# A hybrid decoder block on one core: the recurrence's loads issued by ScalarE's queue, and the first transfers in another order

## The chip, the core and the metric

The kernel runs on one core of one Trainium2 chip. A core has TensorE (matrix products, written into the eight banks of PSUM), VectorE, ScalarE, GpSimd and SyncE, each with an instruction stream of its own that is worked off in order, and 16 DMA engines that move data between the chip's main memory and the on-chip memory (SBUF). An instruction that moves data is issued from an engine's stream: it waits there for its semaphores, hands the transfer over, and the engine goes on. The metric is the device time of one execution in microseconds (us), lower is better.

## What is computed

One layer on 1024 tokens of width 1024, all in float32: a norm, one input projection, two groups of heads (attention and a gated recurrence), an output projection, a norm, a gated feed-forward part, a last norm. Cut to what matters here:

```python
def rmsnorm(x, w):
    y = x * lax.rsqrt(jnp.mean(x * x, axis=-1, keepdims=True) + NORM_EPS)
    return y * w

u = rmsnorm(h, norm1_w[l])                       # (1, 1024, 1024)
proj = jnp.einsum('bsd,de->bse', u, w_in[l])     # 3584 columns: qa ka va | qb fb ib gb

# group B: 4 heads, state 128x128, chunked
f = lb + (1.0 - lb) * jax.nn.sigmoid(f_logit);  key = 1.0 - f;  qf = jax.nn.silu(q)
S_t = diag(f_t) S_{t-1} + key_t i_t^T;          o_t = S_t^T qf_t
o = o * lax.rsqrt(jnp.mean(o * o, axis=-1) + NORM_EPS)
yb = o * norm_w * jax.nn.silu(g)

h = h + concat(ya, yb) @ w_out;  h = h + ffn(rmsnorm(h, norm2_w));  return rmsnorm(h, final_norm_w)
```

## The kernel before

The kernel does every large product in three reduced-precision parts (each operand is split into a high part `wh` and a rest `wl`), and arranges the large products in Strassen's scheme (seven products in place of eight, hence the sums of halves on VectorE). TensorE has work for nearly the whole span; everything else is made to keep it supplied.

**Who sets the order.** The kernel's code does not issue instructions: `P.op` and `P.flex` record operations with their cost, their reads and their writes, and `Prog.schedule` then lists them engine by engine by their class (`P.cls`, a lower number goes first) and by the length of what still hangs on them. Changing one operation's queue or class can so move any other. Each transfer is recorded by `dma(...)` (L267 to L272), in the kernel before always on SyncE's stream (SP). The built program gives every transfer one of eight completion semaphores in turn, so a transfer also waits, at its issue, for the landing of the one that is eight places before it.

**The start** (L658 on). The eight token tiles `xs[0]` to `xs[7]` (128 tokens each, 512 KB, in the tiles `E0`, `E1`, `E14`, `E15`) are loaded. `norm_rows` squares a tile on ScalarE, takes the root on GpSimd and multiplies by the root and by the norm's weights `w1b` in two halves on VectorE. `w1b` (`wh7`, `wl7`) is the weight vector repeated on all 128 partitions, loaded by two transfers that read the same 2 KB for each partition (256 KB each). `blocks` transposes the normed tile on TensorE against `ident` (64 KB, loaded too) and splits it into the operands of the input projection. From the second tile on, `begin` starts the projections `F0` and `K1` early (DENSE lists the order of the twelve projections), with weights loaded into `st0` and `st1`. `consts()` (L627 on) loads masks and works out the recurrence's bounds `lg`, with an exponential on ScalarE.

**The recurrence.** `hgrn(h)` (L840 on) runs four times, in class 0, among the last input projections. Each head loads four arrays that the projections have written to main memory: `f` (`f_d`), the queries (`q_d`), the values `iv` (`i_d`) and, near its end, the gate `gt` (`g_d`), 512 KB each. All heads share the tiles `E14` (f and keys), `E15` (queries) and `E16` (the score matrix `A` and the values); `gt` overwrites `A`. A head ends with eight squares (ScalarE), a root (GpSimd), eight scaled copies (ScalarE), a transposition (TensorE), a product with the gate (VectorE, L305) and two stores to `m_d`. Behind the recurrence comes the attention (class 1), which fetches its operands from `qs_d`, `kh_d`, `kl_d` and `v_d` with SP's transfers, then the output projection, the feed-forward part and the last norm.

Of the kernel before, what the change touches and what calls it, by code (L numbers as in the profile page):

```python
# [246 lines left out]
def hymba_block(ctx: ExitStack, tc: tile.TileContext, x, norm1_w, w_in, lb_logits, hgrn_norm_w, w_out,  # L247
# [15 lines left out]
    def moved(nbytes, run):  # L263

        return nbytes / run * (0.008 + run / 27e3) / 16

    def dma(o, i, nbytes, run=2048):  # L267
        r = [i] if isinstance(i, (View, Buf)) else []
        w = [o] if isinstance(o, (View, Buf)) else []
        gi = i if r else (lambda: i)  # L270
        go = o if w else (lambda: o)
        P.op("SP", 0.5, lambda: nc.sync.dma_start(go(), gi()), r, w, nbytes=moved(nbytes, run))  # L272

# [83 lines left out]
    def bcast(w, n):  # L357
        return bass.AP(tensor=w.tensor, offset=w.offset, ap=[[0, 128], [1, n]])
# [72 lines left out]
    def slot(tag):  # L431
        return whole(P.buf(tag, [128, 512]))
# [219 lines left out]
    def src_of(w):  # L652
        c = COL[w[0]] + int(w[1]) * 256
        return w_in_v[:, :, c:c + 256], w[0] in "QK"
# [4 lines left out]
    for t in range(NT):  # L659
        if t == 0:  # L660
            for i in range(4):
                dma(xs[i], x[i * 128:(i + 1) * 128, :], 128 * D * 4, 4096)
                if i == 0:
                    for k in range(2):
                        dma(w1b[k], bcast(norm1_w[:, k * 512:k * 512 + 512], 512), 128 * 512 * 4)
                    dma(ident, eye, 65536)
        if t == 2:
# [3 lines left out]
        u = us[t % 2]  # L671
        norm_rows(xt, w1b, u, u, "a")
        blocks(t, u, R, "n", tmp4)
# [10 lines left out]
        if t >= 3 and len(leads) < LEAD:  # L684
            w = seq[len(leads)]
            leads[w] = next(begin(R, *src_of(w), "d", slot(T8[4 + len(leads)]), 7))
    consts()

    csn = E(16, [128, 2048])
# [134 lines left out]
    def hgrn(h):  # L824
# [17 lines left out]
        def blocked(v, w):  # L842
            return sub(v, lambda a: a.rearrange("p c (b e) -> p c b e", e=w))
        dma(f, f_d.v(lambda b: b[rs, :], h), 128 * S * 4)
        dma(qc(0, 128), q_d.v(lambda b: b[rs, :].rearrange("p (c e) -> p c e", e=128), h), 128 * S * 4, 512)
        dma(r128(iv), i_d.v(lambda b: b.rearrange("(c p) n -> p c n", p=128)[:, :, rs], h // 2), 128 * S * 4, 512)

# [91 lines left out]
        gt = A  # L939
        dma(gt, g_d.v(lambda b: b[rs, :], h), 128 * S * 4)  # L940
        ss = P.buf("hss", [128, NT])
# [437 lines left out]
```

## Time and profile before

| | us |
|---|---|
| median of 3 runs | 1258.24 (1257.98 to 1258.44) |
| the profiled execution's own time | 1256.03 |
| its span, first to last instruction | 1254.2 |
| TensorE busy in the span | 1212.3 (97%) |
| VectorE busy | 1028.3 (82%) |
| ScalarE busy | 476.9 (38%) |
| GpSimd busy | 112.0 (9%) |

A busy share is a mean over stages with different limits, so the stages are read one by one. Product records on TensorE overlap and their ends are modelled, so "busy" is not the same as full pace. The feed-forward part, from about 625 us to the end, keeps TensorE busy without a gap. The stages in front of it are where its time is lost.

### The profile page before, as it was taken

What the parts mean: (1) busy time and instruction counts of PE and PEld (TensorE: products, weight loads), DVE (VectorE), ACT (ScalarE), POOL (GpSimd) and SP (SyncE); (2) the same over time, 40 slices, a digit from 0 to 9 for tenths busy, and PEclk for the clock granted to TensorE, in tenths of its full rate; (3) what the DMA queues carried; (4) which work ended last, traced back from release to release, by engine and by line L of the source; (5) the groups of instructions that cost most, each with busy time, mean ns of one, the idle gap of its engine ahead of it and who ended that gap; (6) DMA issues with size and microseconds to landing.
All of it is one profiled execution on the core that took longest, in us unless ns stands there. A gap on an engine that the chain in (4) does not pass through costs nothing.

```text
span 1254.2 us, 17960 instructions
## 1 busy us (share of the span) xinstructions
PE 1212.3 (97%) x6244; PEld 1030.7 (82%) x6244; DVE 1028.3 (82%) x2110; ACT 476.9 (38%) x1020; POOL 112.0 (9%) x212
## 2 busy tenths in 40 slices
PE   4999999999998899999999999999999999999997
PEld 4878889888987788987888888888888887888885
DVE  6999989999789999966888676676676769968986
ACT  5642332344327887842722132221222223223222
POOL 1110000101003433420100000000000000000001
PEclk9999999999999999999999999999999999999998
DMA  8434443514468753316223322323322369434433
GB/s 264 133 127 160 176 147 101 182 68 160 132 195 272 203 143 88 93 54 199 79 76 126 118 97 89 126 85 109 126 84 101 112 230 386 170 101 127 135 109 118
DMA packets 132890, 175.57 MB, mean 140 GB/s; under 512 B 18496, under 2 KB 85696, under 8 KB 132800
## 3 DMA queue, kind: packets, MB, share of 16 engines
q1 hardware_dynamic: 132800, 174.43, 42.4%
q8 instruction: 49, 0.80, 0.3%
q14 instruction: 41, 0.34, 0.1%
HBM read 122.76 MB, written 51.64 MB: 139 GB/s over the span
## 4 chain that ended last, share of the span: by engine, by line
PE 78%; DVE 9%; DMA 7%; ACT 2%; issue 1%; SPq 0%; POOL 0%; DVEq 0%; POOLq 0%; ACTq 0%
PE b L280 76%; DVE wl L301 2%; DVE E L301 2%; PE b L1048 2%; DMA st<-in_w_in_dram 1%; DVE E L864 1%; DVE wh L301 1%; PE b L286 1%; DMA m_d<-lm 1%; DMA st<-in_w_out_dram 1%; DMA E<-kl_d 1%; DVE E L305 1%; DMA i_d<-wl 1%; DVE st L301 1%; ACT wh L337 1%
## 5 line engine op out<-in xcount | busy, mean ns | idle before, releaser
L280 PE MATMUL b<-E,wh 128*128 128x512 f32 (+1 forms) x2096 | 643.6, 389 | 5.1 <-ACT wl L337 1.9
L280 PEld LDWEIGHTS b<-E,wh 128*128 128x128 f32 x2096 | 386.3, 188 | 85.5 <-DVE E L301 4.0
L280 PE MATMUL b<-E,wl 128*128 128x512 f32 (+1 forms) x1048 | 403.9, 385 | 0.0
L347 ACT ACTIVATE wh<-st 128x512 fp32r<-128x512 f32 (+1 forms) x207 | 129.4, 629 | 384.6 <-PE b L280 217.1
L301 DVE TENSOR_TENSOR wl<-st,wh 128x512 fp32r<-128x512 f32 (+1 forms) x340 | 229.5, 685 | 5.3 <-ACT wh L347 2.1
L280 PEld LDWEIGHTS b<-E,wl 128*128 128x128 f32 x1048 | 197.1, 188 | 40.7
L301 DVE TENSOR_TENSOR E<-b,E 128x512 f32<-128x512 f32 (+1 forms) x157 | 105.5, 683 | 39.6 <-PE b L280 37.3
L349 DVE TENSOR_SCALAR wh<-st 128x512 fp32r<-128x512 f32 x119 | 50.0, 423 | 88.0 <-PE b L280 84.6
L280 PE MATMUL b<-wl,wh 128*128 128x512 f32 x308 | 119.9, 389 | 0.5 <-DVE wl L301 0.5
L280 PE MATMUL b<-wh,wl 128*128 128x512 f32 x308 | 119.9, 389 | 0.1
L280 PE MATMUL b<-wh,wh 128*128 128x512 f32 x308 | 119.8, 389 | 0.0
L280 PE MATMUL b<-wl,E 128*128 128x256 f32 (+1 forms) x544 | 116.3, 287 | 2.7 <-DVE wl L301 2.6
L301 DVE TENSOR_TENSOR wl<-b,wl 128x512 f32<-128x512 f32 (+2 forms) x139 | 89.6, 651 | 14.8 <-PE b L280 12.2
L280 PE MATMUL b<-E,E 128*128 128x192 f32 (+3 forms) x464 | 99.6, 324 | 2.0 <-DVE E L305 1.0
L301 DVE TENSOR_TENSOR st<-st 128x512 f32<-128x512 f32 x136 | 92.5, 684 | 0.7
L280 PEld LDWEIGHTS b<-wl,E 128*128 128x128 f32 x544 | 88.0, 191 | 5.8 <-DVE wl L301 3.4
L337 ACT ACTIVATE E<-E 128x512 f32<-128x512 f32 (+2 forms) x77 | 54.2, 704 | 93.5 <-DVE E L301 42.5
L280 PE MATMUL b<-wh,E 128*128 128x256 f32 x448 | 89.1, 290 | 0.2 <-DVE wh L301 0.2
L280 PEld LDWEIGHTS b<-E,E 128*128 128x128 f32 x464 | 75.0, 192 | 8.0 <-issue 2.6
L349 POOL TENSOR_SCALAR wh<-st 128x512 fp32r<-128x512 f32 (+1 forms) x16 | 11.1, 692 | 747.6 <-PE b L280 668.3
L280 PEld LDWEIGHTS b<-wh,E 128*128 128x128 f32 x448 | 72.4, 192 | 0.8 <-DVE wh L301 0.4
L280 PEld LDWEIGHTS b<-wl,wh 128*128 128x128 f32 x308 | 57.8, 188 | 13.0 <-DVE wl L301 0.9
(140 smaller groups left out, 1391.7 us busy)
## 6 DMA issues: line engine op xcount, KB each, us to landing
st<-in_w_gate_up_dram SPq DMA_DIRECT2D x22, 1024.0 KB, 5.2
st<-a_d SPq DMA_DIRECT2D x77, 256.0 KB, 2.8
st<-in_w_in_dram SPq DMA_DIRECT2D x16, 1024.0 KB, 5.7
a_d<-E SPq DMA_DIRECT2D x45, 256.0 KB, 2.1
E<-in_w_down_dram SPq DMA_DIRECT2D x44, 256.0 KB, 5.3
E<-in_x_dram SPq DMA_DIRECT2D x8, 512.0 KB, 9.1
E<-qs_d SPq DMA_DIRECT2D x32, 128.0 KB, 3.9
E<-kh_d SPq DMA_DIRECT2D x32, 128.0 KB, 3.6
```

The lines of the kernel that those rows point to most:

```text
L280: nc.tensor.matmul(o(), lt(), rh(), start=st, stop=sp, skip_group_check=True)
L286: nc.tensor.transpose(ov(), iv(), ident())
L301: P.flex(alts, lambda e: ENG[e].tensor_tensor(o(), a(), b(), op=op), [a, b], [o])
L305: lambda e: nc.vector.scalar_tensor_tensor(o(), a(), s(), b(), op0=op0, op1=op1), [a, s, b], [o])
L337: nc.scalar.activation(o(), a(), func, **kw)
L347: nc.scalar.activation(o(), i(), AF.Copy)
L349: ENG[e].tensor_scalar(o(), i(), 1.0, 0.0, op0=OP.mult, op1=OP.add)
L864: nc.vector.copy_predicated(Av, mv, ps()[:, :, a:a + 64].rearrange("p c (b e) -> p c b e", e=w))
L1048: nc.tensor.transpose(ov(), iv(), ident())
```

## The change

Two edits, and what the scheduler makes of them.

1. `dma` takes a queue; the four loads of each of the four heads are recorded on ScalarE's stream in place of SP's.
2. At the start, the first tile, then the two halves of the norm's weights as one row each (2 KB), then `ident`, are recorded in class 0, ahead of all else. A product of a row of ones with each half on TensorE spreads the weights over 128 partitions into a PSUM bank. The first tile multiplies by that bank directly; ScalarE copies it to `w1b` for the other seven. The tiles 1 to 3 come behind. `consts()` gets class 3, the last.

```diff
-    def dma(o, i, nbytes, run=2048):
+    def dma(o, i, nbytes, run=2048, queue="SP"):
...
-        P.op("SP", 0.5, lambda: nc.sync.dma_start(go(), gi()), r, w, nbytes=moved(nbytes, run))
+        e = {"SP": nc.sync, "ACT": nc.scalar}[queue]
+        P.op(queue, 0.5, lambda: e.dma_start(go(), gi()), r, w, nbytes=moved(nbytes, run))
...
-            for i in range(4):
+            P.cls = 0
+            w1p = []
+            dma(xs[0], x[0:128, :], 128 * D * 4, 4096)
+            dma(ident, eye, 65536, 512)
+            rows = [P.buf(x, [1, 512]) for x in T8[:2]]
+            ones = P.buf("ones", [1, 128])
+            for k in range(2):
+                dma(rows[k], norm1_w[:, k * 512:k * 512 + 512], 2048)
+            P.op("DVE", 0.1, lambda: nc.vector.memset(ones(), 1.0), [], [ones])
+            for k in range(2):
+                ps = bank("d")
+                mm([(whole(ps), whole(ones), whole(rows[k]), True, True, 512, 128, True)], [ones, rows[k]], [ps])
+                P.cls = 2
+                act(w1b[k], whole(ps), AF.Copy, 512)
+                P.cls = 0
+                w1p.append(whole(ps))
+            P.cls = 2
+            for i in range(1, 4):
                 dma(xs[i], x[i * 128:(i + 1) * 128, :], 128 * D * 4, 4096)
-                if i == 0:
-                    for k in range(2):
-                        dma(w1b[k], bcast(norm1_w[:, k * 512:k * 512 + 512], 512), 128 * 512 * 4)
-                    dma(ident, eye, 65536)
...
-        norm_rows(xt, w1b, u, u, "a")
+        norm_rows(xt, w1b if t else w1p, u, u, "a")
...
+    P.cls = 3
     consts()
+    P.cls = 2
...
-        dma(f, f_d.v(lambda b: b[rs, :], h), 128 * S * 4)
+        dma(f, f_d.v(lambda b: b[rs, :], h), 128 * S * 4, queue="ACT")
...
-        dma(gt, g_d.v(lambda b: b[rs, :], h), 128 * S * 4)
+        dma(gt, g_d.v(lambda b: b[rs, :], h), 128 * S * 4, queue="ACT")
```

The queries' and the values' loads change in the same way as `f`.

**The start on SP.** Before, the two repeated halves (`wh_70`, `wl_72`) stand third and fourth, the weights of K1 (`st_74`) ahead of `ident`:

```order
L272 DMA E_67<-in_x_dram 128x1024 x2
L272 DMA wh_70<-in_norm_w_dram 128x512
L272 DMA wl_72<-in_norm_w_dram 128x512
L272 DMA st_74<-in_w_in_dram 128x8x256
L272 DMA E_76<-in_x_dram 128x1024
L272 DMA ident<-in_eye_dram 128x128
L272 DMA st_80<-in_w_in_dram 128x8x128
L272 DMA E_76<-in_x_dram 128x1024
L272 DMA E_86<-in_x_dram 128x1024 x2
```

The same place now, on SP, with two rows of 2 KB in place of the two halves and `st_92` for the weights of F0:

```order
L273 DMA E_67<-in_x_dram 128x1024
L273 DMA wh_71<-in_norm_w_dram 1x512
L273 DMA wh_73<-in_norm_w_dram 1x512
L273 DMA ident<-in_eye_dram 128x128
L273 DMA E_67<-in_x_dram 128x1024
L273 DMA E_78<-in_x_dram 128x1024
L273 DMA st_80<-in_w_in_dram 128x8x256
L273 DMA E_78<-in_x_dram 128x1024
L273 DMA E_86<-in_x_dram 128x1024
L273 DMA st_92<-in_w_in_dram 128x8x128
```

`ident` moved from behind K1's weights and the third tile to the fourth place; the second and third tile now stand ahead of K1's weights, and the fifth ahead of F0's.

**The passage from head 2 to head 3.** SP before, where `E_1666<-f_d` is head 3's load, `E_1756<-g_d` head 2's gate, and the rest fetches the attention's operands and its mask:

```order
L272 DMA E_1647<-q_d 128x8x128
L272 DMA E_3099<-qs_d 32x1024 x4
L272 DMA E_3099<-kh_d 32x1024 x3
L272 DMA E_1666<-f_d 128x1024
L272 DMA E_3099<-kh_d 32x1024
L272 DMA E_3163<-in_amask_dram 128x1920
L272 DMA E_3170<-kl_d 32x1024 x4
L272 DMA E_3194<-qs_d 32x1024 x4
L272 DMA E_1756<-g_d 128x1024
```

ScalarE now, around head 2's gate; `E_1766,hss<-b` are the squares, `E_1766<-b,rsh` the scaled copies, `E_1657` head 3's queries:

```order
L338 ACTIVATE E_1657<-E_1657 128x4x64
L338 ACTIVATE E_1766,hss<-b_3154 128x128
L338 ACTIVATE E_1766,hss<-b_3191 128x128
L338 ACTIVATE E_1766,hss<-b_3154 128x128
L338 ACTIVATE E_1766,hss<-b_3191 128x128
L338 ACTIVATE E_1766,hss<-b_3154 128x128
L338 ACTIVATE E_1766,hss<-b_3191 128x128
L338 ACTIVATE E_1766,hss<-b_3154 128x128
L338 ACTIVATE E_1766,hss<-b_3191 128x128
L273 DMA E_1766<-g_d 128x1024
L338 ACTIVATE E_1657<-E_1657 128x4x64
```

And a little ahead of that, around head 3's load of `f` (`E_1676<-b` are the last copies that head 2 writes into the same tile):

```order
L338 ACTIVATE E_1676<-b_3112 128x512
L338 ACTIVATE E_1676<-b_3121 128x512
L273 DMA E_1676<-f_d 128x1024
L348 ACTIVATE wh_3173<-st_2449 128x512
L338 ACTIVATE wl_3204<-b_2884 128x512
```

The gate's load moved from behind SP's fetches of the mask, of `kl_d` and of `qs_d` to right behind the eighth square, and head 3's load of `f` from behind seven of them to right behind head 2's last copies into its tile.

**The bounds of the recurrence.** ScalarE now, at the first results of F0 (`wh_562<-b` is the first sigmoid, `lg<-lg` the exponential of `consts()`):

```order
L338 ACT_TABLE_LOAD
L338 ACTIVATE wh_562<-b_216 128x512
L348 ACTIVATE E_526<-b_570 128x4x128
L338 ACTIVATE wl_593<-b_516 128x512
L338 ACT_TABLE_LOAD
L338 ACTIVATE lg<-lg 128x8
L348 ACTIVATE E_526<-b_604 128x4x128
L338 ACTIVATE wh_651<-b_198 128x512
L348 ACTIVATE wh_666<-st_387 128x512
L348 ACTIVATE E_526<-b_648 128x4x128
L348 ACTIVATE wh_675<-st_607 128x512
L338 ACTIVATE E_681<-b_516 128x512
```

ScalarE before, at the same place (`wh_573<-b` is the first sigmoid):

```order
L347 ACTIVATE wh_567<-st_312 128x512
L337 ACT_TABLE_LOAD
L337 ACTIVATE wh_573<-b_176 128x512
L337 ACTIVATE wl_595<-b_527 128x512
L347 ACTIVATE wh_607<-st_312 128x512
L337 ACTIVATE wh_622<-b_229 128x512
L347 ACTIVATE wh_651<-st_617 128x512
L337 ACTIVATE wh_639<-wh_639 128x512
```

Before, the exponential stood far ahead, under the table that ScalarE loads first; now it has moved in between the sigmoids, with a table load ahead of it and another behind. The program has 11 table loads in place of 9. Elsewhere the places of the four heads among the projections, and the order of the output projection, the feed-forward part and the end, are nearly those of before; the attention's operations are interleaved a little differently.

## Rows read from the trace of the kernel before

**Rows 1.** Stretches: length; PE, PEld, DVE, ACT, POOL busy; granted clock, DMA share, GB/s

```profile
50.00:75.00 25.00, 24.72 (x114) 20.26 (x113) 21.44 (x35) 12.22 (x20) 6.42 (x5) 1.00 0.30 110
...
1075.00:1100.00 25.00, 25.00 (x112) 20.71 (x111) 23.33 (x43) 6.86 (x11) 0.00 (x0) 1.00 0.34 105
...
8.00:26.00 18.00, 10.66 (x58) 9.79 (x59) 14.11 (x27) 9.99 (x20) 2.82 (x5) 1.00 1.09 356
...
336.00:350.00 14.00, 12.12 (x83) 11.00 (x81) 3.45 (x10) 5.70 (x27) 1.98 (x2) 0.88 1.01 276
350.00:400.00 50.00, 46.07 (x340) 43.59 (x341) 48.88 (x143) 24.78 (x70) 9.60 (x19) 1.00 0.70 225
```

**Rows 2.** Timeline of the start: start us, us, engine, instruction [idle before, releaser]

```profile
4.47 1.06 ACT L337 ACTIVATE E<-E 128x1024 f32<-128x1024 f32 x1 [2.47 <-DMA E<-in_x_dram]
...
7.52 0.75 DVE L305 SCALAR_TENSOR_TENSOR E<-E,rsa,wh 128x512 f32<-128x512 f32 x1 [1.72 <-DMA wh<-in_norm_w_dram]
9.18 0.75 DVE L305 SCALAR_TENSOR_TENSOR E<-E,rsa,wl 128x512 f32<-128x512 f32 x1 [0.84 <-DMA wl<-in_norm_w_dram]
...
12.19 0.63 ACT L347 ACTIVATE wh<-st 128x512 fp32r<-128x512 f32 x1 [5.20 <-DMA st<-in_w_in_dram]
...
13.90 3.65 PE L286 MATMUL b<-ident,E 128*128 128x128 f32 x16 [13.90 <-DMA ident<-in_eye_dram]
...
15.53 0.43 DVE L349 TENSOR_SCALAR wh<-st 128x512 fp32r<-128x512 f32 x1 [1.44 <-DMA st<-in_w_in_dram]
...
22.38 1.03 PE L286 MATMUL b<-ident,E 128*128 128x128 f32 x8
```

**Rows 3.** The chain that ended last, at the start: start us, us, what

```profile
18.12 9.85 DMA st<-in_w_in_dram
...
29.68 2.32 PE b L280 x13
```

**Rows 4.** SP's transfers between head 2 and head 3 (timeline)

```profile
331.34 3.55 SPq L272 DMA_DIRECT2D E<-kh_d  x3
335.07 0.34 SPq L272 DMA_DIRECT2D E<-f_d  x1
...
336.40 1.86 SPq L272 DMA_DIRECT2D E<-kl_d  x4
338.36 5.30 SPq L272 DMA_DIRECT2D E<-qs_d  x4
343.91 0.34 SPq L272 DMA_DIRECT2D E<-g_d  x1
```

**Rows 5.** TensorE, VectorE and ScalarE in the same place (timeline)

```profile
331.25 1.79 PE L280 MATMUL b<-E,E 128*128 128x128 f32 x14
...
340.04 0.69 DVE L301 TENSOR_TENSOR E<-E,E 128x512 f32<-128x512 f32 x1 [3.63 <-DMA E<-f_d]
...
341.12 0.26 ACT L337 ACTIVATE E<-b 128x128 f32<-128x128 f32 x1
...
343.02 0.25 ACT L337 ACTIVATION_READ_ACCUMULATOR E<-b 128x1 f32 x1
...
349.96 0.75 DVE L305 SCALAR_TENSOR_TENSOR E<-b,hw,E 128x512 f32<-128x512 f32 x1 [5.65 <-DMA E<-g_d]
```

**Rows 6.** VectorE's waits from 175 to 430 us: us in total, times, longest

```profile
DVE E L305 <- DMA E<-g_d: 5.6, 1, 5.6
DVE E L301 <- DMA E<-f_d: 3.6, 1, 3.6
```

**Rows 7.** ScalarE: its table loads as a group, and rows near them

```profile
L337 ACT ACT_TABLE_LOAD x9 | 11.5, 1283 | 5.2 <-DMA f_d<-wl 4.4 <-PEq L1365 0.7
...
54.39 1.28 ACT L337 ACT_TABLE_LOAD   x1
55.69 0.60 ACT L337 ACTIVATE wh<-b 128x512 f32<-128x512 f32 x1
...
64.26 0.63 ACT L347 ACTIVATE wh<-st 128x512 fp32r<-128x512 f32 x1 [4.40 <-DMA st<-in_w_in_dram]
```

More of the change, by code (lines that the diff above doesn't have):

```diff
@@ L843, in blocked @@
             return sub(v, lambda a: a.rearrange("p c (b e) -> p c b e", e=w))
-        dma(f, f_d.v(lambda b: b[rs, :], h), 128 * S * 4)
-        dma(qc(0, 128), q_d.v(lambda b: b[rs, :].rearrange("p (c e) -> p c e", e=128), h), 128 * S * 4, 512)
-        dma(r128(iv), i_d.v(lambda b: b.rearrange("(c p) n -> p c n", p=128)[:, :, rs], h // 2), 128 * S * 4, 512)
+        dma(f, f_d.v(lambda b: b[rs, :], h), 128 * S * 4, queue="ACT")
+        dma(qc(0, 128), q_d.v(lambda b: b[rs, :].rearrange("p (c e) -> p c e", e=128), h), 128 * S * 4, 512, "ACT")
+        dma(r128(iv), i_d.v(lambda b: b.rearrange("(c p) n -> p c n", p=128)[:, :, rs], h // 2), 128 * S * 4, 512, "ACT")
         def scores(n, g):
```

## The prediction

> **What bounds the kernel now.** Read the table of stretches first: where TensorE is busy all of its 25 us, as at 1075 us, only fewer or faster products could help. It is short of work at the start (10.66 of 18 us from 8 to 26 us) and from 336 to 350 us (12.12 of 14 us, at a mean granted clock of 0.88, so that part of it ran at the lower of the two levels) [rows 1]. The change touches these two places, so each is read from its timeline.
>
> At the start the DMA engines are the limit: their share is 1.09 from 8 to 26 us, at 356 GB/s [rows 1]. What is wanted comes late: the norm's two weight halves at 7.52 and 9.18 us, K1's weights at 12.19, `ident`, for which the first product waits, at 13.90, F0's at 15.53 [rows 2]. The chain of waits goes on through a lot of weights issued at 18.12 that lands 9.85 us later, behind all that is queued, and reaches TensorE at 29.68 [rows 3]. From 336 to 350 us VectorE, the engine nearest to its limit around there, is busy 3.45 of 14 us [rows 1]. It waits 3.63 us for head 3's `f` and 5.65 us for head 2's gate [rows 5], the only loads in its list of waits from 175 to 430 us [rows 6]. SP's rows show why: both loads stand behind fetches for the attention that take 3.55 and 5.30 us to issue [rows 4].
>
> **The change part by part.** *The first transfers.* The two repeated halves are gone. The second arrives 1.66 us after the first [rows 2], and half a megabyte in all would take 1.5 us at the stretch's mean rate [rows 1]; so they hold the engines between 1.5 us and 2 x 1.66 = 3.3 us. Everything behind them lands so much sooner, the chain's lot of weights too, if it is issued as soon as now. Its issue waits until F0's weights are split, for which VectorE must have come as far. Count VectorE and TensorE: the first tile is there at 4.47 [rows 2], the rows and `ident` (64 KB, 0.2 us at that rate) by about 4.7. The spreading product isn't in the trace. The nearest is a float32 product of 128 columns: seven in 14 records take 1.79 us [rows 5], 0.26 us each, so 1.0 us for 512 columns. TensorE is slow then: sixteen transpositions take 3.65 us, eight later ones 1.03 [rows 2], near half the pace. So 2.0 us each: the banks are ready at 6.7 and 8.7, the two multiplications of the first tile start 0.8 and 0.5 us sooner than at 7.52 and 9.18, and the first transposition starts at 8.7 + 0.75 = 9.5 in place of 13.90, 4.4 us sooner. Ends: -0.5 us (VectorE's own chain decides) and -4.4 us (TensorE's start decides). I take -3.3 us, the queue, since the chain [rows 3] runs through the queue, and VectorE, idle 3.9 of these 18 us [rows 1], can make up the rest. The weights' copies (two of ScalarE's 512-column operations) and the products lie ahead of anything that TensorE or ScalarE could else do; they cost nothing unless VectorE then waits for the second tile's weights, which the lower end covers.
>
> *The passage from head 2 to head 3.* Head 3's `f` needs its tile free: its last reads are the products at 331.25 to 333.04 [rows 5]. It was issued at 335.07 [rows 4], so it can go 2.0 us sooner; with its own 4.97 us to VectorE's start at 340.04 [rows 5], VectorE starts at 338.0. The eight squares stand behind this on ScalarE, from 341.12 to 343.27 [rows 5]; they end at 341.2, and the gate goes then rather than at 343.91: 2.7 us sooner. Its 6.05 us to 349.96 [rows 4, 5] unchanged give -2.7 us; with the 4.97 us of `f` it is -3.8 us. I take -3.2 us. Behind it VectorE is busy 48.88 of 50 us [rows 1], so that what reaches it sooner is passed on. Ends: 0 (the loads only land later in the crowd: DMA share 1.01 [rows 1]) and -4.5 us. TensorE lost 1.88 us of idle time there and some 1.7 us by the clock (0.12 of 14) [rows 1], 3.6 us, and what VectorE gains beyond it would have to come out of later waits.
>
> The rule against this part is in the Trainium skill, "DMA: Bandwidth & Descriptors", section "Issuing engines are not separate DMA queues": issuing from several engines saves only the time that the sequencer takes to issue. By it two loads would gain some 0.7 us together (0.34 us each [rows 4]) and the sum would be 1255.1. The trace speaks against it here: the gate waited for its turn to be issued, not only for the engines.
>
> *The other fourteen loads* wait for nobody [rows 6]: 0. Sixteen issues of 0.34 us [rows 4] put 5.4 us on ScalarE, which is busy 24.78 of 50 us there [rows 1]: 0, and at most 1.4 us, one issue a head, if its queries are held up. Where a load must wait for its tile, ScalarE waits too; in the fences of the change what stands behind a load is either the same chain or not due.
>
> *The table loads.* Two more, 1.283 us each [rows 7], 2.6 us of ScalarE between two evictions, about where TensorE now waits on ScalarE's load at 54.39. ScalarE is busy 12.22 of 25 us in that stretch [rows 1] and idle 4.40 us at 64.26 [rows 7]; that covers most. From 0 to 2.6 us; I take 0.5. The Trainium skill, "ScalarE: Activation LUTs", section "What ACT_TABLE_LOAD costs", adds a drain that makes 2.66 us of each switch; by that the upper end would be 5.3 us. Here the load at 54.39 ends at 55.67 and the next operation starts at 55.69 [rows 7], so the trace does not show the drain.
>
> **The sum.** -3.3 - 3.2 + 0.5 = -6.0 us. The profiled execution took 1256.03 us (span 1254.2 and 1.8 around it), so 1250.0 on its own scale; the runs' median, 1258.24, is 2.2 us above it, so 1252.2.
>
> **The rivals.** *Only the start gains.* The gate lands at the same time because the mask and the attention's operands fill the engines (share 1.01 [rows 1]). That is the skill's rule just named, worked out from rows: 1258.24 - 3.3 + 0.5 - 0.3 = 1255.1. For it: the crowd. Against it: SP stood still for 5.30 us just ahead of the gate [rows 4].
>
> *Only the passage gains.* VectorE, or TensorE at half pace, sets the start: -0.5 - 3.2 + 0.5, 1255.0. For it: VectorE works 14.11 of 18 us there [rows 1], and is nearly full afterwards.
>
> *Given back in the attention.* Its operations come in another order, and from 350 to 400 us TensorE lost 3.9 us [rows 1] although VectorE had no time to spare. If a like amount is lost anew, or the mask, now behind head 3's `f`, comes late, both gains shrink to between -2 and +2 us: about 1258.
>
> *Slower.* ScalarE is held by its loads. It may reach head 3's `f` while the 1.79 us of last reads [rows 5] begin, and stand until they end. If the twelve loads of `f`, queries and values each held it so, it would stand 21 us; were half of that to reach VectorE, which has no slack in the recurrence, the time would be 1258.24 - 3.3 + 0.5 + 10.7 = 1266.1. It decides from where ScalarE comes to a load over a microsecond ahead of its tile and an eviction or a copy of queries due now stands behind. Against it: ScalarE is idle half the time, and the order puts loads behind the operations that free their tiles.
>
> **How the numbers follow.** What a measurement here can tell from no change is about 0.2%, 2.5 us: faster is below 1255.7, slower above 1260.8. Both gains, 1248.5 to 1255: 0.58. Only the start: 0.12. Only the passage: 0.09. Given back: 0.14. Slower: 0.07. Faster is so 0.79, the same 0.14, slower 0.07. The range takes in both single gains and the upper ends of both terms with some of their costs, and leaves out half of the case "given back" and the slower one: 1247.5 to 1257.0.
>
> **What would show it.** First product (spreading) by about 5 us and first transposition near 9.5; the lot of weights that landed at 27.97 landing near 24.7; TensorE's steady supply from about 26.4 in place of 29.68. Head 3's `f` issued within a microsecond of its tile's last read, the gate right behind the eighth square, VectorE's two waits of 3.63 and 5.65 us down to some 6 us together, and no clock below 1.00 there. ScalarE's two extra table loads without a longer wait of TensorE. Wrong would be: the gate's landing moved by less than its issue, new waits of VectorE on ScalarE in heads 0 to 2, or a loss between 350 and 550 us that grows by as much as the passage gains.

## The result, and the profile after

The changed kernel takes 1273.2 us in the median (1271.95 to 1274.36) against 1258.11 (1257.32 to 1258.44): ratio 1.0125, interval 1.0109 to 1.0141. It is 15.1 us slower, and the prediction, 1252.2 with a range up to 1257.0, was wrong in sign. The profiled execution took 1272.95 us, its span is 1271.2.

The stretches, to be held against [rows 1], with the same columns:

```profile
8.00:26.00 18.00, 13.88 (x76) 11.48 (x76) 16.08 (x30) 12.76 (x26) 4.25 (x8) 1.00 1.03 329
336.00:350.00 14.00, 12.72 (x97) 11.64 (x96) 5.49 (x13) 5.31 (x27) 1.98 (x2) 1.00 0.64 188
350.00:400.00 50.00, 39.85 (x286) 37.97 (x285) 39.56 (x113) 16.61 (x38) 6.65 (x11) 0.93 0.59 185
```

Both places that the change was forecast to help are fuller: TensorE works 13.88 of 18 us at the start (10.66 before) and 12.72 of 14 us in the passage (12.12), where the clock stays at 1.00 (0.88). The loss stands behind: from 350 to 400 us TensorE works 39.85 us in place of 46.07, VectorE 39.56 in place of 48.88, and the granted clock falls to 0.93. The page shows a second loss that no stretch of gaps contains, in its busy times of PE, PEld, DVE, ACT and POOL:

```profile
PE 1225.0 (96%) x6248; PEld 1030.5 (81%) x6248; DVE 1034.0 (81%) x2131; ACT 477.4 (38%) x1016; POOL 110.2 (9%) x200
```

TensorE is busy 12.7 us longer than before (1212.3) with four more products. So there are two questions: what stopped TensorE behind 350 us, and why its products take longer.

The passage and what follows, from the timelines of SP, ScalarE, VectorE and TensorE (start us, us, engine, instruction, [idle before, releaser]; `ACTq` is a transfer issued by ScalarE's stream):

```profile
338.29 0.69 DVE L302 TENSOR_TENSOR E<-E,E 128x512 f32<-128x512 f32 x1 [2.78 <-DMA E<-f_d]
340.04 0.37 ACTq L273 DMA_DIRECT2D E<-g_d  x1
340.10 8.70 SPq L273 DMA_DIRECT2D E<-qs_d  x4
347.45 1.41 DVE L306 SCALAR_TENSOR_TENSOR E<-b,hw,E 128x512 f32<-128x512 f32 x2 [4.88 <-DMA E<-g_d]
350.67 0.68 ACT L338 ACTIVATE E<-E 128x512 f32<-128x512 f32 x1 [5.65 <-PE b L281]
351.24 0.41 SPq L273 DMA_DIRECT2D st<-in_w_out_dram  x1
351.75 0.98 SPq L273 DMA_DIRECT2D m_d<-E  x2
360.97 0.38 ACTq L273 DMA_DIRECT2D E<-i_d  x1
361.45 1.06 ACT L348 ACTIVATE E<-st 128x1024 fp32r<-128x1024 f32 x1 [10.10 <-DMA m_d<-E]
362.41 0.61 ACT L338 ACTIVATE E<-E 128x512 f32<-128x512 f32 x1
363.08 4.10 PE L281 MATMUL b<-E,E 128*128 128x192 f32 x12 [7.83 <-ACT E L338]
```

The rows of before that answer to the second half (SP's and ScalarE's timelines):

```profile
347.70 0.41 SPq L272 DMA_DIRECT2D st<-in_w_out_dram  x1
350.74 1.86 SPq L272 DMA_DIRECT2D m_d<-E  x2
355.89 0.37 SPq L272 DMA_DIRECT2D E<-i_d  x1
...
355.98 0.64 ACT L337 ACTIVATE E<-E 128x512 f32<-128x512 f32 x1 [1.85 <-DVE E L873]
356.55 1.06 ACT L347 ACTIVATE E<-st 128x1024 fp32r<-128x1024 f32 x1
```

Read them in order of time. `f` reaches VectorE at 338.29 (340.04 before) and the gate at 347.45 (349.96), both sooner; whether the queue made them so is asked at the end. ScalarE issues the gate at 340.04, and in the same instant SP comes to four fetches of the attention's queries and stands there for 8.70 us, until after the gate has landed (VectorE starts on it at 347.45). The megabyte of the output weights (`in_w_out_dram`), some places behind them, goes out at 351.24, 3.54 us later than before, with the stores of head 2's result to `m_d` right on its heels. Head 3's values (`i_d`) overwrite the tile that these stores read, so their load waits for the stores. Before, the load waited on SP; now it waits on ScalarE, which does nothing from 351.35 to 360.97. Behind it stand a split of the output weights (L348) and the second half of head 3's scaled queries (L338), for which TensorE waits 7.83 us. Before, the copy stood ahead of the split and had no load in front. Why the stores take so long shows in the list of transfers from 335 to 362 us (KB each, us from issue to landing), of after:

```profile
m_d<-E SPq DMA_DIRECT2D x2, 256.0 KB, 8.5
```

and of before:

```profile
m_d<-E SPq DMA_DIRECT2D x2, 256.0 KB, 3.9
```

The same 256 KB need 8.5 us behind the megabyte and 3.9 us where it had a lead of three. TensorE comes back at the lower clock (0.51 from 363 to 367 us, 1.00 before):

```profile
363.00:367.00 4.00, 3.92 (x13) 3.92 (x13) 1.69 (x3) 0.02 (x1) 0.00 (x0) 0.51 0.28 85
```

### The profile page after: what moved, and what is told of

The parts are those of the page before. It is cut to its first block, busy times and chain, and to the rows that moved or that the text cites. A ratio compares the mean times of both kernels' runs of the same rounds, so it can differ in the third digit from the quotient of the medians.

```text
span 1271.2 us, 17936 instructions
## 1 busy us (share of the span) xinstructions
PE 1225.0 (96%) x6248; PEld 1030.5 (81%) x6248; DVE 1034.0 (81%) x2131; ACT 477.4 (38%) x1016; POOL 110.2 (9%) x200
## 4 chain that ended last, share of the span: by engine, by line
PE 62%; DMA 3%; DVE 2%; ACT 1%; issue 1%; SPq 0%; POOL 0%; DVEq 0%; POOLq 0%; ACTq 0%
PE b L281 60%; PE b L1064 2%; DMA st<-in_w_out_dram 1%; DMA m_d<-lm 1%; DVE E L302 1%; DMA E<-in_w_down_dram 0%; DVE wl L302 0%; DMA st<-a_d 0%; DVE wh L1027 0%; DVE E L306 0%; PE b L287 0%; ACT E L338 0%; DMA st<-in_w_gate_up_dram 0%; SPq L273 0%; ACT E L348 0%
## 5 line engine op out<-in xcount | busy, mean ns | idle before, releaser
L348 ACT ACTIVATE wh<-st 128x512 fp32r<-128x512 f32 (+1 forms) x202 | 126.2, 628 | 376.7 <-PE b L281 224.5
L338 ACT ACTIVATE E<-E 128x512 f32<-128x512 f32 (+2 forms) x77 | 54.1, 703 | 93.4 <-DVE E L302 42.0
L350 POOL TENSOR_SCALAR wh<-st 128x512 fp32r<-128x512 f32 x17 | 11.4, 671 | 766.3 <-PE b L281 655.5
```

The lines of the kernel that those rows point to most:

```text
L338: nc.scalar.activation(o(), a(), func, **kw)
L348: nc.scalar.activation(o(), i(), AF.Copy)
L350: ENG[e].tensor_scalar(o(), i(), 1.0, 0.0, op0=OP.mult, op1=OP.add)
```

## The experiments

Every ratio is against the kernel before on the same chip, with its 95% interval. Moves of one instruction are written as operation numbers taken from the schedule and put behind another; the words say which they are.

### Each edit alone

With the loads back on SP, the start's edit alone:

```diff
-        dma(f, f_d.v(lambda b: b[rs, :], h), 128 * S * 4, queue="ACT")
+        dma(f, f_d.v(lambda b: b[rs, :], h), 128 * S * 4)
```

(the queries, the values and the gate likewise).

> The changed kernel with the recurrence's sixteen loads back on SyncE's stream; the edited start stays. Theory 1 (ScalarE is held at head 3's values load): the 9.62 us in which ScalarE stands idle until that load is issued at 360.97 us are gone, and with them the wait of TensorE (7.83 us before 363.08); what is left against the kernel before is the start (about -1 us, as heads 0 to 2 of the changed kernel run about 1 us earlier) and whatever makes the large products slower (219 instead of 222 products per 50 us, about +5 us over the run): 1260 to 1264 us. Theory 2 (the edited start itself costs the time): 1270 us or more. Theory 3 (the slower products come with the loads on ScalarE's queue): 222 products per 50 us again and 1256 to 1258 us; if they come with the start's edit they stay at 219.

And the reverse, the kernel before with the four loads on ScalarE's stream:

> The kernel before with only the four loads of each head recorded on ScalarE's stream; the start as before. Theory 1 (ScalarE is held at head 3's values load): the hold of about 9 us shows again near 350 to 362 us, the passage ahead of it gains about 2.5 us, and the attention's beginning loses up to 6 us more in its new order: 1262 to 1270 us. If the slower products belong to the start's edit (other tile addresses), the feed-forward part has 222 products per 50 us; if they belong to the queue, 219, and the time is 1268 to 1274 us. Rival (the hold needs the start's edit too): no hold, 1254 to 1257 us.

Measured: 1.0081 [1.0054, 1.0108] for the start alone, 1.0085 [1.0056, 1.0114] for the loads alone. Each is slower by itself. The loads alone show the hold:

```profile
361.76 0.38 ACTq L273 DMA_DIRECT2D E<-i_d  x1
362.24 1.06 ACT L348 ACTIVATE E<-st 128x1024 fp32r<-128x1024 f32 x1 [10.47 <-DMA m_d<-E]
```

The start alone has no such wait; over 4 of its 10 us go in the feed-forward part, which the change doesn't touch: from the 2500th product before the last to the end it takes 583.4 us, the kernel before 579.2 (578.5 with the loads alone).

### Why the products are slower

Two kernels, 350 us of the feed-forward part without a gap on TensorE: length, PE busy and its records, granted clock, DMA share, GB/s. Before:

```profile
650.00:1000.00 350.00, 350.00 (x1539) 1.00 0.31 106
```

After:

```profile
650.00:1000.00 350.00, 350.00 (x1525) 1.00 0.31 107
```

Same work, same clock, same load on the DMA engines, 0.9% fewer products. What differs are addresses: a tile is reserved in SBUF when it is first used, so the new tile `ones` (512 bytes) and the tile `mhalf` (32 bytes), before reserved ahead of `E0` and now behind it, shift the others. The 512 bytes by themselves leave every remainder modulo 256 as it was; the small tiles of 32 bytes, which now lie between other large tiles, change it. From the built programs, with the remainder modulo 256:

```
        before        after         every operand tile on one grid
E0      16544  160    17024  128    20608  128
E1      37024  160    29856  160    28800  128
E7     197024  160   187296  160   176768  128
E14     62144  192    54464  192    36992  128
wh7     24736  160    82304  128    63616  128
wh8    149920  160    25248  160    67712  128
```

The distance from one start of a 512-column product to the next (the trace's records) is 226 to 227 ns for most, and mostly 232 to 236 where one of the two tiles read in turn is E14, before. Summed over some 3900 of these distances, what goes beyond 226.65 ns is 3.8 us before and 10.8 us after, where E0, E14 and wh7 lie apart from the rest. With the loads alone, whose tiles lie as before, it is 3.7, with the start alone 10.7. The first form of this theory took tiles to be alike if they agree modulo 64 bytes; three small tiles were widened to 64 bytes a partition, which puts all operands on a multiple of 64:

```diff
-            self.t = self.prog.pools[self.pool].tile(self.shape, self.dt, name=self.tag, bufs=1)
+            wide = [128, 16] if self.tag in ('mhalf', 'ssa', 'hw') else self.shape
+            t = self.prog.pools[self.pool].tile(wide, self.dt, name=self.tag, bufs=1)
+            self.t = t[:, :self.shape[1]] if wide is not self.shape else t
```

> The changed kernel with three small tiles (mhalf, ssa, hw) padded to 64 bytes, so that every tile which TensorE reads in a large product begins at a multiple of 64 bytes; the order of every engine's work is unchanged. In the kernel before all such tiles but E14 lie 32 bytes off a multiple of 64, in the changed kernel all but E0, E14 and wh7. Address theory (products whose operands lie partly on and partly off the 64-byte grid run slower): 222 products per 50 us in the feed-forward part instead of 219, 1265 to 1269 us (5 to 8 us less than 1273.2). Rival (the pace comes from what else runs beside the products, the queues or the order): 219 per 50 us and 1272 to 1275 us.

Measured: 1.0119 [1.009, 1.0148], and an excess of 9.5 us: that form fell. E0, E1 and wh7 to wh9 were still 64 or 128 bytes off the others modulo 256. The second form, alike to a larger step: all large tiles are reserved first, one behind the other, in whole multiples of 512 bytes, and every instruction keeps its order.

```diff
+        if self.prev is None and pool == "sb" and int(np.prod(shape[1:])) >= 128:
+            prog.large.append(self)
...
-        for i in self.schedule():
+        order = self.schedule()
+        for b in self.large:
+            b()
+        for i in order:
```

> The changed kernel with all its large tiles (512 bytes or more) reserved first, so that they all begin 128 bytes off a multiple of 512; the order of every engine's work is unchanged. In the kernel before the tiles that TensorE's products read are alike to a multiple of 256 bytes, all but E14; in the changed kernel E0, E14, wh7 and their partners fall apart; the run with three padded tiles, which still had E0, wh7, wh8 and wh9 64 bytes off the others, stayed at 219 to 220 products per 50 us. Address theory, in its second form (products run at full pace when their operands are alike to a multiple of 128 bytes): 220.6 products per 50 us at full pace is 226.7 ns from start to start, which is 3924 products x 2.7 ns = 10.8 us less than now: 1261 to 1264 us where the changed kernel takes 1273. Rival (addresses don't matter, the pace is that of the queues or the order): 219 per 50 us and 1271 to 1275 us.

> The kernel before with all its large tiles reserved first, so that they all begin 128 bytes off a multiple of 512; the order of every engine's work is unchanged. Address theory: the products of E14 and E7, which take 232 to 236 ns from start to start where all others take 227, come to 227 too: 3.8 us less, ratio 0.997. Rival (addresses don't matter): ratio 1.000.

Measured: 1.0076 [1.0046, 1.0106] for the changed kernel, 0.999 [0.9975, 1.0005] for the kernel before. The excess is 2.0 and 2.1 us, and the changed kernel gets through more than before did:

```profile
650.00:1000.00 350.00, 350.00 (x1546) 1.00 0.30 105
```

So the addresses alone cost the changed kernel 6 to 9 us: the excess falls by 8.8 us, and the ratio by 0.49% from the first runs of the changed kernel (6.2 us) and by 0.63% (7.9 us) from 1.0139 [1.0126, 1.0153], which it gave on another chip; either difference is known to some 0.33%, 4 us. The kernel before has an excess of 3.8 us itself, so that between the two kernels the pace makes 7.0 us. That the kernel before gains by the grid, as was expected from its own fall of 1.7 us, is not shown.

> The changed kernel once more, beside three variants and the kernel before on one chip, because the chips of the last two calls spread by 3 us from run to run. All theories: ratio 1.0125 as first measured (1.010 to 1.015), 15 us.

That the addresses do it is shown, since `after_grid` changes nothing else; the rule of the remainders is not shown to be whole. With each product of the trace laid beside its tiles in the built program, before, 3549 distances whose moving and weight tiles all agree modulo 256 are 227.2 ns in the mean, and 299 with E14 in them 232.7. After, 1199 distances with an odd tile are 232.1 ns, but the 2651 where all agree are still 228.2 and hold 4.2 of the 10.8 us.

### What the hold consists of

First suspicion: the values' load alone holds ScalarE. It went back to SP, the other three loads stayed.

```diff
-        dma(r128(iv), i_d.v(lambda b: b.rearrange("(c p) n -> p c n", p=128)[:, :, rs], h // 2), 128 * S * 4, 512, "ACT")
+        dma(r128(iv), i_d.v(lambda b: b.rearrange("(c p) n -> p c n", p=128)[:, :, rs], h // 2), 128 * S * 4, 512)
```

> The changed kernel with only the values' loads (i_d, one a head) back on SyncE's stream; f, the queries and the gate stay on ScalarE's. Theory 1 (ScalarE is held at head 3's values load): ScalarE's query copies run at about 352 us instead of 361, TensorE's gap of 7.83 us goes, 1262 to 1265 us (1273.2 less 8 to 11). Rival (the stores to m_d that land 8.5 us after their issue are what the chain needs, on whichever queue the load waits): the copies come early, but the next head's products wait for the values all the same, 1270 us or more. The attention's loss near 400 to 415 us and the products' pace of 219 per 50 us stay in both.

Measured: 1.0119 [1.0092, 1.0146]. ScalarE still stands, now for the output weights themselves, and TensorE with it (ScalarE's and TensorE's timelines):

```profile
358.11 1.06 ACT L348 ACTIVATE E<-st 128x1024 fp32r<-128x1024 f32 x1 [7.73 <-DMA st<-in_w_out_dram]
...
359.74 4.21 PE L281 MATMUL b<-E,E 128*128 128x192 f32 x12 [5.46 <-ACT E L338]
```

Not the load, then, but what is late on SP. Second: only the copy of the queries (operation 1711) is in the wrong place. In ScalarE's order the values' load (1687) and the split of the output weights (2947) go behind it:

```diff
+        order = self.schedule()
+        for i in [1687, 2947]:
+            order.remove(i)
+        k = order.index(1711) + 1
+        order[k:k] = [1687, 2947]
```

> The changed kernel with one thing moved in ScalarE's order: head 3's second query copy stands ahead of the values' load and of the split of the output projection's first weights (st0), where in the changed kernel it stands behind both; nothing else moves. Theory (the loss at 351 to 363 us is that copy's place behind two waits, for the stores to m_d and for the weights): the copy runs near 353.5 us, TensorE's gap of 7.83 us goes, and 1263 to 1266 us come out where the changed kernel takes 1273 (7.8 us less, and up to 2 us of half clock behind the gap). Rival (the values, landed only at about 364 us, are needed at once, so the wait moves behind the next products): 1269 us or more, with a new gap before 365 us.

Measured: 1.0117 [1.0086, 1.0148]. The copy runs at 354.73, but TensorE then waits for the next thing behind the hold, the output weights by way of VectorE:

```profile
354.73 0.64 ACT L343 ACTIVATE E<-E 128x512 f32<-128x512 f32 x1 [2.13 <-DVE E L894]
361.03 0.38 ACTq L278 DMA_DIRECT2D E<-i_d  x1
...
362.59 1.23 DVE L307 TENSOR_TENSOR E<-st,E 128x1024 fp32r<-128x1024 f32 x1 [4.56 <-ACT E L353]
...
364.65 1.62 PE L286 MATMUL b<-E,E 128*128 128x192 f32 x4 [4.41 <-DVE E L885]
```

Third: SP itself is held by the gate. By the built program, the gate's load is a place in the turn of the eight semaphores ahead of the four fetches, and the second of these takes the semaphore that the gate uses and waits there for the gate's landing. With the gate alone back on SP:

> The changed kernel with only the gate's loads (g_d, one a head) back on SyncE's stream; f, the queries and the values stay on ScalarE's. In the changed kernel SyncE stands 8.70 us at four loads of qs_d (340.10 to 348.80), the second of which shares a completion semaphore with the gate's load that ScalarE issued and that lands at 347.4. Theory (SyncE's queue is held by ScalarE's load through the shared semaphores, and so sends the 1 MB of weights 3.5 us later, 351.24 instead of 347.70): with the gate on SyncE's own stream the weights are sent at 347 to 348 us again, ScalarE's wait at the values' load is 2 to 5 us instead of 9.6, the attention's beginning is as in the kernel before, and the time is 1263 to 1267 us. Rival (ScalarE's load of the values alone makes the wait): the weights come early but the wait stays near 9 us, 1270 us or more.

Measured: 1.009 [1.0062, 1.0118]. SP's and ScalarE's timelines:

```profile
339.94 1.74 SPq L273 DMA_DIRECT2D E<-qs_d  x4
...
345.86 0.41 SPq L273 DMA_DIRECT2D st<-in_w_out_dram  x1
349.67 1.86 SPq L273 DMA_DIRECT2D m_d<-E  x2
...
354.25 0.38 ACTq L273 DMA_DIRECT2D E<-i_d  x1
```

The same four fetches take 1.74 us in place of 8.70, the weights go out 5.4 us sooner, and the values' load, still on ScalarE, at 354.25 in place of 360.97. That is the mechanism by its own row; the stores behind the weights land in 3.4 us again. On the grid the same edit gives 1.0041 [1.0028, 1.0055], against 1.0076 with the gate on ScalarE, where the hold stands as in the first trace (TensorE waits 7.63 us); the forecast was 0.999 to 1.004.

> The changed kernel with the gate's loads back on SyncE's stream and the large tiles reserved first at one offset. Theory (two causes, added: SyncE held by the gate's load through the shared semaphores, and the tiles' offsets): both are gone, so 8.5 us less than the run with the gate alone moved back (ratio 1.0090), 0.999 to 1.004. Rival (a third cost of the loads on ScalarE's queue): 1.005 or more.

The last experiment on it keeps every load on ScalarE and SP's hold too, and takes away only what stands behind it: the output weights' load goes ahead of the four fetches (operation 2946; on the grid).

```diff
+        for i in [2946]:
+            order.remove(i)
+        k = order.index(1845) + 1
+        order[k:k] = [2946]
```

> The changed kernel with the large tiles at one offset and one entry moved in SyncE's order: the load of the output projection's first weights (1 MB into st0) stands ahead of the four loads of qs_d at which SyncE stands, where in the changed kernel it stands behind them and the four of kh_d. Theory (what SyncE sends late is the cause): the stores to m_d no longer stand behind 1 MB and land about 4 us after their issue instead of 8.5, ScalarE's stand at the values' load shrinks from 9.6 to 4 to 5 us, TensorE's gap from 7.8 to 2 or 3 us, and the ratio is 1.001 to 1.004 (the changed kernel with its tiles at one offset had 1.0076). Rival (the load's place on ScalarE is the cause): gap 7 us or more, 1.007 or more. It can also go wrong because the gate's load, issued at the same time, lands later beside the 1 MB.

Measured: 1.0034 [1.0022, 1.0047]. SP's, ScalarE's and TensorE's timelines:

```profile
339.73 0.57 SPq L282 DMA_DIRECT2D st<-in_w_out_dram  x1
348.54 1.69 SPq L282 DMA_DIRECT2D E<-qs_d  x4
...
352.68 0.92 SPq L282 DMA_DIRECT2D m_d<-E  x2
...
356.64 0.44 ACTq L282 DMA_DIRECT2D E<-i_d  x1
...
358.81 2.22 PE L290 MATMUL b<-E,E 128*128 128x192 f32 x12 [2.72 <-ACT E L347]
```

and from the list of transfers:

```profile
m_d<-E SPq DMA_DIRECT2D x2, 256.0 KB, 3.3
```

SP still stands until 348.54, but the stores land in 3.3 us, the values' load goes at 356.64 and TensorE waits 2.72 us instead of 7.63 on the grid (7.83 without). From 1.0076 to 1.0034 are 0.42%, 5.3 us, known to some 4 us: that is the price of what the hold makes late.

### What is left

After addresses and hold, 0.34% stays, 4 us. Four kernels, all on the grid, went after it. The start's edit without the loads:

> The edited start alone (the recurrence's loads on SyncE's stream, as in the run with the start alone, ratio 1.0081) with the large tiles reserved first at one offset. Theory (the edited start costs nothing by itself; its loss was the products' pace, 8.7 of the 10.7 us that the products took over full pace): ratio 0.999 to 1.002, 1 us of gain at the start included. Rival (the start's new order costs 3 to 4 us in the attention's beginning as well): 1.002 to 1.005.

Measured: 1.0014 [1.0005, 1.0022], so even with its addresses mended the start's edit gains nothing in the end. With `f` alone on ScalarE as well:

> The edited start, the large tiles at one offset, and of the recurrence's loads only f_d on ScalarE's stream. Theory (ScalarE's issue pays only where no later load of SyncE's shares its semaphore while it is under way, and f_d's load lands before SyncE comes back to it): the wait for f_d at the passage from head 2 to head 3 is 1 us shorter than the 3.63 us of before, and the ratio is 0.996 to 1.001. Rival (any load on ScalarE's queue shifts SyncE's turn): SyncE stands 3 us or more at a load of qs_d or kh_d between 330 and 345 us, ratio over 1.003.

Measured: 1.0027 [1.0011, 1.0043], slower than was expected, with SP not held; the intervals do not tell it from 1.0014. The last head's gate was the next suspect: ScalarE issues it behind its own work at 399.57 (392.51 on SP before), and the next output weights are sent just behind it and are the longest transfer in the chain that ended last, 10.67 us. After, ScalarE's and SP's timelines and the chain:

```profile
399.57 0.34 ACTq L273 DMA_DIRECT2D E<-g_d  x1
...
400.84 0.40 SPq L273 DMA_DIRECT2D st<-in_w_out_dram  x1
...
400.84 10.67 DMA st<-in_w_out_dram
```

Its gate went back to SP, on top of the weights moved ahead (`queue="SP" if h == 3 else "ACT"`):

> As the run with the weights sent first, and the last head's gate load back on SyncE's stream (the other fifteen loads stay on ScalarE's). Theory: that load is issued near 392 us of the old count again instead of behind ScalarE's eight squares, so that it no longer meets the weights sent at 400 us, and the attention's beginning loses 3 to 6 us less: ratio 0.997 to 1.001. Rival (the attention's beginning varies for other reasons): the same ratio as with the weights sent first alone, within 0.002.

Measured: 1.0033 [1.002, 1.0046], no difference from 1.0034; a striking row was not a cause. The same with the old start:

> The kernel before, with fifteen of the sixteen loads on ScalarE's stream (the last gate stays on SyncE's), the weights sent first and the large tiles at one offset; the start as before. If the passage's gain of 2.5 us survives and nothing else is lost: ratio 0.995 to 0.998, better than both kernels. If ScalarE's queue only moves waits: 0.999 to 1.004.

Measured: 1.0045 [1.0027, 1.0063]. So the loads on ScalarE bring nothing even with their hold taken away. Where the last 4 us sit row by row stays open. The start's edit without the loads accounts for some 2 of them (1.0014); that the attention's new order is behind this is only argued. The loads with the old start cost 0.45% and both edits together 0.33%, so the two shares do not simply add up, and no run parts them further.

The passage's wait can be shortened without ScalarE: in the kernel before, on the grid, the gate ahead of the last two fetches in SP's order, and then `f` one fetch sooner as well. The grid alone ran again beside the later kernels.

```diff
+        for i in [1653]:
+            order.remove(i)
+        k = order.index(1652) + 1
+        order[k:k] = [1653]
```

> The kernel before with the large tiles at one offset and, in SyncE's order, head 2's gate load ahead of the last two of the four qs_d loads at which SyncE stands 5.30 us (338.36 to 343.66); nothing else moves. Theory (the passage's wait is set by the load's place in its queue): the gate is sent about 340.8 us when its tile is free, lands 2.5 to 3 us earlier, TensorE's gaps near 343 to 351 us (1.26 and 1.00, and the half clock) shrink, and the ratio is 0.997 to 0.999. Rival (the gate lands no earlier beside the mask's 960 KB, or the attention's beginning gives the gain back): 1.000.

> As the run with the gate first, and head 3's f load one place earlier too, ahead of the third kh_d load. Theory: another 0.5 to 1 us at the wait for f (3.63 us before 340.04), ratio 0.996 to 0.999. Rival: no difference between the two.

> The kernel before with its large tiles at one offset once more. By the products' sum 1.7 to 3.8 us less: ratio 0.997 to 0.9985. Rival (the gain is lost in the waits of the attention's beginning): 1.000.

Measured: 0.9991 [0.9978, 1.0005], 0.9989 [0.9974, 1.0003] and 1.0000 [0.9982, 1.0017]. None is shown to beat the kernel before. The gate sent 4.8 us sooner (339.07 for 343.91) reached VectorE only 1.7 us sooner (348.23) than in the first trace of the kernel before, and no sooner than in its trace on the grid (348.09):

```profile
348.23 0.75 DVE L314 SCALAR_TENSOR_TENSOR E<-b,hw,E 128x512 f32<-128x512 f32 x1 [5.31 <-DMA E<-g_d]
```

## Why the prediction was wrong, step by step

**The start, -3.3 us: right in direction, too large.** TensorE's first transposition stands at 8.25, sooner than the 9.5 forecast, and the rows behind it show why little came of it (TensorE's and VectorE's timeline of after):

```profile
4.57 3.75 PE L281 MATMUL b<-wh,ones 1*128 1x512 f32 x4 [4.57 <-DMA wh<-in_norm_w_dram]
6.73 0.75 DVE L306 SCALAR_TENSOR_TENSOR E<-E,rsa,b 128x512 f32<-128x512 f32 x1 [0.86 <-POOL rsa L374]
8.25 1.11 PE L287 MATMUL b<-ident,E 128*128 128x128 f32 x4
...
15.99 1.94 PE L287 MATMUL b<-ident,E 128*128 128x128 f32 x8 [2.33 <-DVE E L306]
```

The spreading products take 3.75 us, close to the 4.0 that were worked out, and VectorE starts at 6.73 instead of 7.52. But VectorE is then busy 16.08 of 18 us, TensorE waits for it at 15.99, and from 26 to 50 us TensorE works 22.81 of 24 us (23.65 before): VectorE's own work, not the queue, sets the start. That was the lower end, -0.5 us. TensorE comes out of the same short wait for VectorE in the last projections at 179.42 in place of 180.17, 0.75 us ahead, with 1.3 us of slower products already behind it; but with the start alone, and the same slower products, at 181.34. On the grid the same wait ends at 178.71 to 179.78 with the new start (six traces, 179.3 in the mean) and at 179.14 to 180.85 with the old one (five, 180.0). So the start gained between nothing and 2 us, some 0.7 by the means. I had taken the queue because the chain of waits ran through it.

**The passage, -3.2 us: not shown to come from the gate's place in the queue.** The first pair of traces looks like the forecast: `f` 1.75 us and the gate 2.5 us sooner, VectorE's two waits 2.78 and 4.88 us (7.7 together; "some 6" was forecast), no clock below 1.00 up to 350 us. But the gate was issued 3.87 us sooner (340.04 for 343.91), so its landing moved by less than its issue, which the prediction had listed as a sign of being wrong: the 6.05 us from issue to VectorE that it took as unchanged became 7.41. And the gate comes as early with the loads on SP: at 348.53 with the start alone, at 348.09 and 348.50 in the kernel before on the grid, once with the clock at 1.00 in the passage, once at 0.93. The kernel before and the changed kernel, both on the grid (SP's, ScalarE's and VectorE's timelines):

```profile
341.84 0.34 SPq L277 DMA_DIRECT2D E<-g_d  x1
348.09 0.75 DVE L310 SCALAR_TENSOR_TENSOR E<-b,hw,E 128x512 f32<-128x512 f32 x1 [5.62 <-DMA E<-g_d]
...
340.32 0.35 ACTq L278 DMA_DIRECT2D E<-g_d  x1
348.16 1.41 DVE L311 SCALAR_TENSOR_TENSOR E<-b,hw,E 128x512 f32<-128x512 f32 x2 [5.31 <-DMA E<-g_d]
```

Issued 1.5 us sooner, the gate reaches VectorE no sooner. TensorE is fuller in the passage with the loads on ScalarE (12.72 to 12.92 of 14 us in three traces, 10.23 to 12.12 in five with them on SP), so a part of the gain may be real, but it did not come by the gate's landing. At the gate that is the rival "only the start gains", to which the prediction gave 0.12; why the gate lands when it does, no run shows. By the rule that the prediction took from the Trainium skill, "DMA: Bandwidth & Descriptors", section "Issuing engines are not separate DMA queues", only the time of issue would be saved, 0.34 us a load. The first pair of traces, 2.5 us for the gate, seemed to speak against it; the traces on the grid agree with it, with no gain at the gate.

**The step that failed is "the other fourteen loads: 0".** It rested on the sentence that "what stands behind a load is either the same chain or not due". At head 3's values that is false: the second copy of the queries stands behind the load, is due, and does not need it. I read the fences of the order for head 3's `f` and the gate, and took the other loads from the list of VectorE's waits of before, where loads on SP could not delay ScalarE. The slower rival named the right engine and "a copy of queries due now", at a chance of 0.07, but priced twelve small holds from the last reads of TensorE, 1.79 us each. In its place the trace shows one hold of 9.6 us, worth 5.3 us of the time, from a chain that crosses queues: gate on ScalarE, semaphore, SP, output weights, stores, values on ScalarE. The front text states the turn of eight semaphores; the prediction never asked whose turn the gate would share on its new queue.

**The table loads, +0.5 us.** Eleven against nine, as forecast, 1.283 us each:

```profile
L338 ACT ACT_TABLE_LOAD x11 | 14.1, 1283 | 7.5 <-DMA f_d<-wl 4.4 <-DVE E L302 2.3 <-PEq L1381 0.7
```

No wait of TensorE on them was found.

**What the sum had no term for: 6 to 9 us of addresses.** It counted the tile `ones` only by its product. Where the tiles come to lie costs more than any wait of the change. The trace of before held a hint, E14's products at 232 to 236 ns beside 227, but not what a new tile would do. This term alone, 7.0 us between the two kernels, is larger than the whole forecast gain.

**"A loss between 350 and 550 us that grows by as much as the passage gains"** was listed as what would make the prediction wrong, and it is what came: from 350 to 400 us TensorE works 6.2 us less.

The account, from runs: addresses 6 to 9 us, the hold 5.3 us, some 4 us not placed; together 15 to 18, against 15.1 and 17.0 in the two sets of runs of the changed kernel. The three are steps between ratios as the causes are undone in turn, so that they add up by construction and any gain at the start is already in them; each ratio is known to 0.1 to 0.3%, 1 to 4 us.

## What to carry to other kernels

Before a load is moved to a computing engine's stream, ask two things of its new place: what stands behind it that is due while it waits, and which other queue's transfers take their turn on the same completion semaphore. Count a sooner landing, not a sooner issue, and in more than one trace. An edit that adds or moves a tile moves all the tiles behind it; compare the pace of untouched products in a stage without gaps before looking for a wait.

## What the runs showed of the hardware

- The pace of TensorE's 512-column products depends on where the tiles lie that they read: before, 227.2 ns in the mean from start to start where all tiles read in turn agree modulo 256 bytes, and 232.7 ns where one of them is 32 bytes off (E14). Summed beyond 226.65 ns, 3.8 us before, 10.8 after, 2.0 with all tiles on a grid of 512 bytes; multiples of 64 bytes were not enough (9.5). Agreement from one product to the next is not the whole rule: after, such distances are 228.2 ns. What in the chip causes it, no run shows.
- A transfer on one engine's stream can hold another engine's: four fetches took 8.70 us on SP while the gate was under way on ScalarE's stream, and 1.74 us with the gate on SP.
- A gate issued sooner did not reach VectorE sooner: sent at 339.07 (gate first), 340.32 (the changed kernel), 341.84 and 343.38 us (the kernel before, twice), all on the grid, it reached VectorE at 348.23, 348.16, 348.09 and 348.50.
- Products of 128 by 192 run at about half pace behind the gap: twelve take 4.10 us at a granted clock of 0.51 (after, 363.08) and 2.22 us at a granted clock of 1.00 behind the shorter gap of 2.72 us, with the output weights moved ahead. So the long gap on TensorE cost 1.9 us more than its length.
